# One hybrid layer on one core: h of the mLSTM branch transposed by VectorE through DRAM, gate stores on ScalarE's queue, row 5 of the modulation through yb's tiles, decay rows loaded a head ahead

## The chip, the core and the metric

The kernel runs on one core of a Trainium2 chip. A core has TensorE (PE, matrix products and transposes), VectorE (DVE), ScalarE (ACT), GpSimd (POOL) and SyncE (SP); each works through its own queue in order, and they wait for one another by semaphores. SP, ACT and POOL can issue DMA transfers, which 16 DMA engines carry out. The metric is the device time of one execution in microseconds (us), less is better; the comparison is by medians of repeated runs.

## The reference

One layer of a language model in float32: sequence 512, width 1024. A feed-forward part, then a mixing part with two branches (an mLSTM of 4 heads, and attention of 16 heads with a forget gate), then a second feed-forward part. Nine modulation rows come from a small product with w_ada. Cut to what matters here:

```python
def mlstm_chunkwise(q, k, v, i_pre, f_pre):
...
def forgetting_attention(q, k, v, f_pre, q_g, k_g):
...
    q = jnp.moveaxis(rms_norm(q, q_g), 1, 2)
    k = jnp.moveaxis(rms_norm(k, k_g), 1, 2)
...
    F = jnp.moveaxis(jnp.cumsum(jax.nn.log_sigmoid(f_pre.astype(f32)), axis=1), 1, 2)
...
        logits = jnp.einsum('bhqd,bhkd->bhqk', q_blk, k).astype(f32) * scale + (F_blk[..., :, None] - F[..., None, :])
        logits = jnp.where(k_pos[None, :] <= q_pos[:, None], logits, -jnp.inf)
        p = jax.nn.softmax(logits, axis=-1)
...
def hybrid_layer(...):
    mod = jax.nn.silu(c) @ w_ada + b_ada
    sh1, sc1, g1, sh2, sc2, g2, sh3, sc3, g3 = [m[:, None, :] for m in jnp.split(mod, N_MOD, axis=-1)]

    u = rms_norm(x, ffn1_norm_g) * (1 + sc1) + sh1
    x = x + 0.5 * g1 * swiglu(u, ffn1_w_in, ffn1_w_out)

    u = rms_norm(x, mix_norm_g) * (1 + sc2) + sh2
    z = u @ w_mix + b_mix
...
    y_a = jax.nn.sigmoid(o_m) * rms_norm(h_m, mlstm_norm_g).reshape(B, S, MLSTM_V).astype(x.dtype)
    y_b = forgetting_attention(...)
    merged = jax.nn.sigmoid(g_a) * (y_a @ w_branch_a) + jax.nn.sigmoid(g_b) * (y_b @ w_branch_b)
    x = x + g2 * (merged @ w_out)

    u = rms_norm(x, ffn2_norm_g) * (1 + sc3) + sh3
    x = x + 0.5 * g3 * swiglu(u, ffn2_w_in, ffn2_w_out)
    return x
```

The sizes are D = 1024, SEQ = 512, 4 mLSTM heads of 128 (keys) and 256 (values), 16 attention heads of 64, feed-forward width 2816. The columns of w_mix give, in this order, q, k, v and o of the mLSTM, its two gates, q, k, v and the gate of the attention, and the gates g_a and g_b of the two branches.

## The kernel before

All 512 tokens stay on the chip. Activations of a gemm lie transposed (128 features x 512 tokens, 8 tiles uh/ul). Each float32 product is made of three passes on rounded halves, high and low (`mm3`, lines 139 to 143): a weight tile raw of 512 KB is loaded by SP (`raw`, L106, a ring of three), rounded by ACT to wh (L116), and VectorE makes the rest wl (L118). The first two matmuls of an `mm3` in `gemm_stat` read wh only, the third reads wl.

The mixing part, roughly 390 to 830 us, runs in stages. First the gates and the mLSTM's q and k (`qk_conv`), with v of the mLSTM (`v_mlstm`: g banks in PSUM are evacuated into vf, L1066, and split into vm). Beside it, row 5 of the modulation is summed: `ada_row` (L305) loads eight raw tiles of w_ada and accumulates each, times a column of c, into two tiles yb6 and yb7 (L320). Then the mLSTM: `mlstm_w` makes the weights W of a head, `mlstm_h` its output hn, normalised and scaled (L1135), and stored to DRAM as h_d (L1136), 128 KB at a time. Then the attention, 16 heads, in a software pipeline over n (run, the loop over 18): `fox_s(n)` makes the scores (S: loads of the decay row A, L1257; Am, L1260; reductions L1271 and L1275; exponentials L1279), `fox_o(n - 2)` the product with the values (L1327), `fox_p(n - 1)` the probabilities: scaling by 1/sum (L1289), transposes (L1297), and their split into Ph (ACT, L1295) and Pl (DVE, L1296). `fox_t(p)` makes q and k of a pair of heads: for the first group by TensorE from tk, for the others from fT, which VectorE has transposed in blocks of 32 x 32 (L1176) and DRAM and `blocks` (L1141) have put together.

Between these steps stand generators of gemm work: `advance(fill, n)` takes n steps. A step is half a gemm of 24 matmuls. While heads 0 to 11 run, the fill is `fox_qkv` of the next group and `gate` (L1365: tanh of a gate's gemm, stored to g_d by SP one step later, L1367). While heads 12 to 15 run, the fill is `y_a(m)`, m = 0 to 7: the gemm of o, its tanh th (L1342), the load of a 512 x 128 piece of h_d as ht (L1344), four transposes of ht by TensorE (L1347), ya = scaled copy of their bank (ACT, L1349), and ya times (th + 1) (DVE, L1350).

The order on each engine is not the program's order: a scheduler places instructions by readiness in its own model, and the program's order is its priority. PSUM has four banks g for gemms and four banks t for the rest.

## Time and profile before

| | |
|---|---|
| median of 3 runs | 1313.94 us (1313.6 to 1314.72) |
| the profiled execution | 1315.71 us |
| its span, from first to last instruction | 1313.9 us |
| granted TensorE clock, mean | 0.999 |
| TensorE matmul busy | 1298.1 us |
| VectorE, ScalarE busy | 959.3 us, 632.0 us |
| DMA traffic | 260.49 MB, 198 GB/s |

In the answers of the trace, a group of instructions is one line: line of the code, engine, operation, out<-in by the program's names, shape and count, then busy time in us and mean in ns of one, then idle time of the engine before them and what ended it. A window is start:end and length, the busy time of PE, PEld (weight loads), DVE, ACT and POOL with counts, the granted clock, the share of DMA and GB/s. A chain is read from the top down: start, length, what the end of the window waited for at that time.

### The profile page before, as it was taken

What the parts mean: (1) busy time and instruction counts of PE and PEld (TensorE: products, weight loads), DVE (VectorE), ACT (ScalarE), POOL (GpSimd) and SP (SyncE); (2) the same over time, 40 slices, a digit from 0 to 9 for tenths busy, and PEclk for the clock granted to TensorE, in tenths of its full rate; (3) what the DMA queues carried; (4) which work ended last, traced back from release to release, by engine and by line L of the source; (5) the groups of instructions that cost most, each with busy time, mean ns of one, the idle gap of its engine ahead of it and who ended that gap; (6) DMA issues with size and microseconds to landing.
All of it is one profiled execution on the core that took longest, in us unless ns stands there. A gap on an engine that the chain in (4) does not pass through costs nothing.

```text
span 1313.9 us, 17822 instructions
## 1 busy us (share of the span) xinstructions
PE 1298.1 (99%) x6297; PEld 1088.0 (83%) x6297; DVE 959.3 (73%) x1748; ACT 632.0 (48%) x1055; POOL 37.2 (3%) x57
## 2 busy tenths in 40 slices
PE   7999999999999999999999999999999999999998
PEld 6788888887889878888888888878898888888887
DVE  6877777478688887888889685668567556635787
ACT  5633232355476665557575675334372223223651
POOL 1000000000010101000000000003000000000000
PEclk9999999999999999999999999999999999999999
DMA  9999978464855635535446482777539768634574
GB/s 290 277 330 304 324 258 285 128 192 154 301 138 146 201 110 149 163 110 154 127 106 174 101 215 77 235 218 236 182 113 322 265 221 279 221 104 133 170 265 150
DMA packets 231562, 260.49 MB, mean 198 GB/s; under 512 B 40544, under 2 KB 172288, under 8 KB 231472
## 3 DMA queue, kind: packets, MB, share of 16 engines
q1 hardware_dynamic: 231088, 259.27, 63.6%
q8 instruction: 50, 0.82, 0.3%
q14 instruction: 40, 0.33, 0.1%
q0 software_dynamic: 320, 0.06, 0.0%
q10 hardware_dynamic: 64, 0.02, 0.0%
HBM read 220.43 MB, written 38.87 MB: 197 GB/s over the span
## 4 chain that ended last, share of the span: by engine, by line
PE 84%; DVE 6%; DMA 5%; ACT 2%; issue 1%; SPq 1%; ACTq 0%; POOL 0%; DVEq 0%; POOLq 0%
PE g L143 22%; PE g L142 22%; PE g L141 22%; PE t L142 4%; PE t L141 4%; PE t L143 4%; PE g L925 1%; PE t L1327 1%; DMA raw<-in_w_mix_dram 1%; DVE wl L118 1%; PE t L1297 1%; DMA raw<-in_w_ada_dram 1%; DMA raw<-in_w_branch_b_dram 1%; ACT wh L116 1%; PE t L1268 1%
## 5 line engine op out<-in xcount | busy, mean ns | idle before, releaser
L116 ACT ACTIVATE wh<-raw 128x1024 fp32r<-128x1024 f32 (+2 forms) x246 | 249.1, 1017 | 361.6 <-PE g L142 124.3
L118 DVE TENSOR_TENSOR wl<-raw,wh 128x1024 fp32r<-128x1024 f32 (+2 forms) x246 | 287.4, 1171 | 144.6 <-ACT wh L116 122.8
L141 PE MATMUL g<-uh,wh 128*128 128x512 f32 (+1 forms) x880 | 340.7, 387 | 0.0
L143 PE MATMUL g<-uh,wl 128*128 128x512 f32 (+1 forms) x880 | 339.4, 386 | 0.0
L142 PE MATMUL g<-ul,wh 128*128 128x512 f32 (+1 forms) x880 | 339.2, 385 | 0.0
L143 PEld LDWEIGHTS g<-uh,wl 128*128 128x128 f32 x880 | 165.3, 188 | 33.6
L141 PEld LDWEIGHTS g<-uh,wh 128*128 128x128 f32 x880 | 165.4, 188 | 32.9 <-issue 0.5
L142 PEld LDWEIGHTS g<-ul,wh 128*128 128x128 f32 x880 | 165.4, 188 | 32.5
L141 PE MATMUL g<-wh,uh 128*128 128x512 f32 (+1 forms) x256 | 97.0, 381 | 1.5 <-DVE vf L1066 1.3
L143 PE MATMUL g<-wh,ul 128*128 128x512 f32 (+1 forms) x256 | 96.6, 377 | 0.0
L142 PE MATMUL g<-wl,uh 128*128 128x512 f32 (+1 forms) x256 | 96.5, 377 | 0.1
L320 DVE SCALAR_TENSOR_TENSOR acc<-raw,ccol,acc 128x1024 f32<-128x1024 f32 (+1 forms) x56 | 56.8, 1031 | 36.3 <-DMA raw<-in_w_ada_dram 36.2
L142 PE MATMUL t<-wl,A 128*128 128x512 f32 x176 | 68.6, 390 | 0.0
L141 PE MATMUL t<-wh,A 128*128 128x512 f32 x176 | 68.6, 390 | 0.0
L141 PEld LDWEIGHTS g<-wh,uh 128*128 128x128 f32 x256 | 48.1, 188 | 10.8 <-DVE vf L1066 1.7
L143 PEld LDWEIGHTS g<-wh,ul 128*128 128x128 f32 x256 | 48.2, 188 | 9.1
L142 PEld LDWEIGHTS g<-wl,uh 128*128 128x128 f32 x256 | 48.2, 188 | 8.9 <-DVE wl L118 0.5
L143 PE MATMUL g<-yh,wl 128*128 128x512 f32 x128 | 50.2, 392 | 0.2
L141 PE MATMUL g<-yh,wh 128*128 128x512 f32 x128 | 49.8, 389 | 0.0
L142 PE MATMUL g<-yl,wh 128*128 128x512 f32 x128 | 49.8, 389 | 0.0
L1279 ACT ACTIVATE S<-S,mn 128x128 f32<-128x128 f32 (+1 forms) x64 | 35.5, 555 | 19.7 <-DVE mn L1275 9.8
L436 ACT ACTIVATE A<-E 128x768 fp32r<-128x768 f32 x22 | 18.6, 846 | 54.7 <-DVE E L435 54.7
(373 smaller groups left out, 2245.8 us busy)
## 6 DMA issues: line engine op xcount, KB each, us to landing
raw<-in_ffn_w_in_dram SPq DMA_DIRECT2D x82, 512.0 KB
raw<-in_w_ada_dram SPq DMA_DIRECT2D x56, 512.0 KB
raw<-in_w_mix_dram SPq DMA_DIRECT2D x46, 512.0 KB
sa<-in_ffn_w_out_dram SPq DMA_DIRECT2D x22, 512.0 KB
sb<-in_ffn_w_out_dram SPq DMA_DIRECT2D x44, 256.0 KB
ws<-sa SPq DMA_DIRECT2D x22, 512.0 KB
ws<-sb SPq DMA_DIRECT2D x44, 256.0 KB
raw<-ws SPq DMA_DIRECT2D x44, 256.0 KB
```

Of the source, the lines that this page charges most:

```text
L116: nc.scalar.activation(hi, src, AF.Copy)
L118: self.last_lo = nc.vector.tensor_tensor(lo, src, hi, op=SUB)
L141: pin(mm(ps, lh, rh, start=start, stop=False))
L142: pin(mm(ps, lh, rl, start=False, stop=False))
L143: self.last_mm = pin(mm(ps, ll, rh, start=False, stop=stop))
L320: nc.vector.scalar_tensor_tensor(a, r[:, s], c, a, op0=MUL, op1=ADD)
L436: nc.scalar.activation(A1[:, 0:3, :], E[:, 0:3, :], AF.Copy)
L925: pin(nc.tensor.matmul(acc_ps[b], (wl if p == 1 else wh)[:, b % 2, s], self.ul[k] if p == 2 else self.uh[k], start=k == 0 and p == 0, stop ...
L1268: nc.tensor.matmul(ps[:, :w], q[:, s], k[:, :w], start=True, stop=False)
L1279: nc.scalar.activation(S[:, ws], S[:, ws], AF.Exp, scale=-1.0, bias=m, accum_out=sm[:, qb:qb + 1])
L1297: tr = lambda b, c, qb, kb: nc.tensor.transpose(b[:, c:c + P], S[:, P_OFF[qb] + kb * P:P_OFF[qb] + (kb + 1) * P], self.ident)
L1327: nc.tensor.matmul(po[:, q0:], vt[:, kb, i, :], Px[:, o:o + T - q0], start=n == 1, stop=n == 8)
```

## The change

`ada_early` takes the place of `ada_row` for row 5: 16 loads of 128 x 512 into yb0 to yb3 (two alternating pairs), not through raw; its products on VectorE are tied behind the last weight split or the last Wl. The 16 scalings of hn go to ACT; VectorE then transposes each 128 x 512 tile in blocks of 32 x 32, in place, and 256 KB are stored one step later. `ht_load` brings a piece of h, transposed, by four loads in 128-byte pieces (`blocks`), one m ahead; y_a has no TensorE transposes, and its product on VectorE comes a step later. A gate's store is issued by ACT right behind the tanh. `fox_s(h)` loads the decay row of head h + 1. `fox_t(0)` and `fox_t(1)` come earlier among the fill steps.

```diff
@@ -320,6 +320,30 @@
...
+            yield
+
+    def ada_early(self, v, yb, bank):
+
+        nc, A, V = self.nc, self.A, self.nc.vector
+        parts = [(yb[6], slice(0, 512)), (yb[7], slice(512, D))]
+        def load(k):
+            r = yb[2 * (k % 2):2 * (k % 2) + 2]
+            for t, (a, s) in zip(r, parts):
+                nc.sync.dma_start(t, A["w_ada"][0, k * P:(k + 1) * P, v * D + s.start:v * D + s.stop])
+            return r
+        r = load(0)
+        yield
+        for k in range(NK):
+            now, r = r, load(k + 1) if k + 1 < NK else None
+            c = self.ccol[:, k:k + 1]
+            with self.tc.issue_after(self.tie.ins):
+                for t, (a, s) in zip(now, parts):
+                    if k == 0:
+                        V.tensor_scalar(a, t, c, None, op0=MUL)
+                    else:
+                        V.scalar_tensor_tensor(a, t, c, a, op0=MUL, op1=ADD)
+            if k == NK - 1:
+                self.ada_sum(v, parts, lambda: yb[5][0:2, :], bank)
             yield
 
     def ada_sum(self, v, parts, new_row, bank):
@@ -1104,17 +1128,18 @@
...
-            nc.vector.tensor_tensor(Wl[:, ws], W[:, ws], Wh[:, ws], op=SUB)
+            self.tie = nc.vector.tensor_tensor(Wl[:, ws], W[:, ws], Wh[:, ws], op=SUB)
         self.W[h] = (Wh, Wl)
 
     def mlstm_h(self, h, ip):
         nc, sp = self.nc, self.sp
         (Wh, Wl), (vh, vl) = self.W[h], self.vt[h]
         ss = sp.tile([P, NT], F32, name=self.nm("hs"), tag="hs", bufs=2)
-        hs = []
+        hs, h2s = [], []
         for tb in range(NT):
             if tb % 2 == 0:
                 h2 = ip.tile([P, 2, 256], F32, name=self.nm("hn"), tag="bc", bufs=4)
+                h2s.append(h2)
             ps = self.tbank()
             for sb in range(tb + 1):
                 o = W_OFF[sb] + (tb - sb) * P
@@ -1132,8 +1157,13 @@
         nc.vector.tensor_scalar(v, ss, 1.0 / 256, EPS, op0=MUL, op1=ADD)
         r = self.rsqrt(v, NT)
         for tb in range(NT):
-            nc.vector.tensor_scalar(hs[tb], hs[tb], r[:, tb:tb + 1], None, op0=MUL)
-            nc.sync.dma_start(self.h_d[tb * P:(tb + 1) * P, h * 256:(h + 1) * 256], hs[tb])
+            nc.scalar.activation(hs[tb], hs[tb], AF.Copy, scale=r[:, tb:tb + 1])
+            if tb % 2:
+                t = h2s[tb // 2].rearrange("p b n -> p (b n)")
+                nc.vector.transpose(t, t)
+                self.post(1, lambda t=t, b=tb - 1: nc.sync.dma_start(
+                    self.h_d[b * P:(b + 2) * P, h * 256:(h + 1) * 256].rearrange("(b p) n -> p b n", p=P),
+                    t.rearrange("p (b n) -> p b n", b=2)))
 
     def blocks(self, t, src):
 
@@ -1253,8 +1283,11 @@
 
         nc, sp = self.nc, self.sp
         q, k, kl = (t[h % 2] for t in self.qkt[h // 2])
-        A0 = ip.tile([P, T], F32, name=self.nm("A0"), tag="bc", bufs=4)
-        nc.sync.dma_start(A0, self.A_d[h:h + 1, :].to_broadcast([P, T]))
+        def bring(h):
+            t = ip.tile([P, T], F32, name=self.nm("A0"), tag="bc", bufs=4)
+            nc.sync.dma_start(t, self.A_d[h:h + 1, :].to_broadcast([P, T]))
+            return t
+        A0 = bring(h) if h == 0 else self.A0
         Am = ip.tile([P, T], F32, name=self.nm("Am"), tag="bc", bufs=4)
...
@@ -1278,6 +1311,8 @@
             ws = slice(o, o + (qb + 1) * P)
             nc.scalar.activation(S[:, ws], S[:, ws], AF.Exp, scale=-1.0, bias=m, accum_out=sm[:, qb:qb + 1])
         self.S[h] = (S, sm)
+        if h < 15:
+            self.A0 = bring(h + 1)
 
     def fox_p(self, h, ip):
 
@@ -1331,23 +1366,28 @@
         nc.vector.tensor_tensor(self.yb[2 * g + pr][rows, :], po[rows, :], tmp[rows, :], op=ADD)
 
 
+    def ht_load(self, m, ip):
+        t = ip.tile([P, T], F32, name=self.nm("ht"), tag="tok", bufs=4)
+        self.blocks(t, self.h_d[:, m * P:(m + 1) * P])
+        self.ht.append(t)
+
     def y_a(self, m, ap, ip):
         nc = self.nc
+        if m == 0:
+            self.ht = []
+            self.ht_load(0, ip)
         ps = self.gbank()
         w = self.w_stat(self.A["w_mix"][0], OM + m * P)
         self.gemm_stat(ps, w, 0, T, range(0, 4))
         yield
+        if m + 1 < NK:
+            self.ht_load(m + 1, ip)
         self.gemm_stat(ps, w, 0, T, range(4, 8))
         th = self.tmp(ip, "th")
         nc.scalar.activation(th, ps, AF.Tanh, scale=0.5, bias=self.hom[:, m:m + 1])
-        ht = ip.tile([P, NT, P], F32, name=self.nm("ht"), tag="tok", bufs=4)
-        nc.sync.dma_start(ht, self.h_d[:, m * P:(m + 1) * P].rearrange("(b p) n -> p b n", p=P))
-        b = self.tbank()
-        for tb in range(NT):
-            nc.tensor.transpose(b[:, tb * P:(tb + 1) * P], ht[:, tb, :], self.ident)
         ya = ap.tile([P, T], F32, name=self.nm("ya"), tag="qk", bufs=16)
-        nc.scalar.activation(ya, b, AF.Copy, scale=self.hmg[:, m:m + 1])
-        nc.vector.scalar_tensor_tensor(ya, th, 1.0, ya, op0=ADD, op1=MUL)
+        nc.scalar.activation(ya, self.ht[m], AF.Copy, scale=self.hmg[:, m:m + 1])
+        self.post(1, lambda: nc.vector.scalar_tensor_tensor(ya, th, 1.0, ya, op0=ADD, op1=MUL))
         self.ya[m] = ya
         yield
 
@@ -1364,7 +1404,7 @@
             th = self.tmp(ip, "tg")
         nc.scalar.activation(th, ps, AF.Tanh, scale=0.5, bias=self.hgg[:, 8 * i + m:8 * i + m + 1])
         if not keep:
-            self.post(1, lambda: nc.sync.dma_start(self.g_d[8 * i + m], th))
+            nc.scalar.dma_start(self.g_d[8 * i + m], th)
         yield
 
 
@@ -1534,15 +1574,17 @@
         self.qk = [None] * 8
...
-        early = self.ada_row(5, lambda: self.yb[6:8], lambda: self.yb[5][0:2, :], self.tbank)
+        early = self.ada_early(5, self.yb, self.tbank)
         self.ada = (s for v in (6, 7) for s in self.ada_row(v, new, row, self.gbank))
         with tc.tile_pool(name="gates", bufs=1) as mp:
...
+            next(early)
             for m in range(4, 8):
                 ps = self.gbank()
                 w = self.w_stat(w_mix, m * P)
+                self.tie = self.last_lo
                 next(early)
                 self.gemm_stat(ps, w, 0, T)
                 if m == 7:
@@ -1579,12 +1621,12 @@
             for h0, n, fill in ((0, 3, with_gates(self.v_mlstm(1, ip, ip), 1)), (2, 4, with_gates(self.fox_qkv(0, ip), 3))):
                 for f, h in ((self.mlstm_w, h0), (self.mlstm_w, h0 + 1), (self.mlstm_h, h0), (self.mlstm_h, h0 + 1)):
                     f(h, ip)
-                    for _ in range(n):
+                    for i in range(n):
                         advance(fill, 1)
                         if f == self.mlstm_w and h < 2:
                             next(early, None)
-                    if f == self.mlstm_h and h == 2:
-                        self.fox_t(0, yp)
+                        if f == self.mlstm_h and h == 2 and i == 1:
+                            self.fox_t(0, yp)
                 advance(fill, 99)
             for n in range(18):
                 if n % 4 == 0 and n < 16:
@@ -1594,11 +1636,14 @@
                 last = n >= 12
                 if n < 16:
                     self.fox_s(n, ip)
-                    advance(fill, 4 if n == 0 else 3 if n == 1 else 1 if last else 2)
+                    advance(fill, 4 if n == 0 else 1 if last else 2)
+                if n == 1:
+                    self.fox_t(1, yp)
+                    advance(fill, 1)
                 if n >= 2:
                     self.fox_o(n - 2, ip)
                     advance(fill, 1)
-                if n % 2 and n < 13:
+                if n % 2 and 1 < n < 13:
                     self.fox_t((n + 1) // 2, yp)
                     if n == 11:
                         self.fox_t(7, yp)
```

The last part of the attention stage on ScalarE, before (names: wh is the weight of the y_a gemm whose raw it reads, g a gemm's bank, S the scores of head 13, th the tanh):

```order
L116 ACTIVATE wh_7653<-raw_7651 128x1024
L1292 ACTIVATE Ph_7674<-ident 128x128
L1279 ACTIVATE S_7588,sm_7590<-S_7588,mn_7589 128x128
L116 ACTIVATE wh_7754<-raw_7752 128x1024
L1279 ACTIVATE S_7588,sm_7590<-S_7588,mn_7589 128x256
L1279 ACTIVATE S_7588,sm_7590<-S_7588,mn_7589 128x384
L116 ACTIVATE wh_7837<-raw_7835 128x1024
L1279 ACTIVATE S_7588,sm_7590<-S_7588,mn_7589 128x512
L1342 ACTIVATE th_7626<-g_7565,hom 128x512
L1349 ACTIVATE ya_7635<-t_7630,hmg 128x512
```

There the weights of the next three gemms (raw_7651, raw_7752, raw_7835) are split ahead of the tanh of y_a(1), whose bank is g_7565. After the change, from the tanh of y_a(1) (g_7569) on:

```order
L1389 ACTIVATE ya_7719<-ht_7619,hmg 128x512
L1387 ACTIVATE th_7636<-g_7569,hom 128x512
L1365 ACTIVATE yt_7649<-t_7640 64x512
L116 ACTIVATE wh_7655<-raw_7653 128x1024
L1312 ACTIVATE S_7723,sm_7725<-S_7723,mn_7724 128x256
L1328 ACTIVATE Pl_7810<-ident 128x128
L1312 ACTIVATE S_7723,sm_7725<-S_7723,mn_7724 128x384
L1312 ACTIVATE S_7723,sm_7725<-S_7723,mn_7724 128x512
L1389 ACTIVATE ya_7802<-ht_7700,hmg 128x512
L1387 ACTIVATE th_7717<-g_7652,hom 128x512
L1365 ACTIVATE yt_7780<-t_7771 64x512
L116 ACTIVATE wh_7754<-raw_7752 128x1024
```

The weight of y_a(2) (raw_7653) now stands behind the tanh of y_a(1), and that of y_a(3) (raw_7752) behind the tanh of y_a(2), each with yt between.

On VectorE, in the same place, before (S_7588 is head 13, Am_7855 head 15):

```order
L1275 ISA S_7588,mn_7589<-t_7608,A_1438_7584,mn_7589 128x384
L1275 ISA mn_7589 128x1
L118 TENSOR_TENSOR wl_7755<-raw_7752,wh_7754 128x1024
L118 TENSOR_TENSOR wl_7838<-raw_7835,wh_7837 128x1024
L1286 RECIPROCAL sm_7590<-sm_7590 128x4
L1260 TENSOR_TENSOR Am_7855<-A_1494_7853,maskF 128x512
L1289 TENSOR_SCALAR S_7588<-S_7588,sm_7590 128x128
L1350 SCALAR_TENSOR_TENSOR ya_7635<-th_7626,ya_7635 128x512
L1331 TENSOR_TENSOR yb_3661<-t_7638,yt_7647 64x512
L1289 TENSOR_SCALAR S_7588<-S_7588,sm_7590 128x256
L1289 TENSOR_SCALAR S_7588<-S_7588,sm_7590 128x384
L1289 TENSOR_SCALAR S_7588<-S_7588,sm_7590 128x512
```

Behind head 13's last reduction come the low halves of the weights of y_a(3) and y_a(4). After (S_7591 is head 13, wl_7573 the weight of y_a(1)):

```order
L1308 ISA S_7591,mn_7592<-t_7611,A_1411_7482,mn_7592 128x384
L1308 ISA mn_7592 128x1
L1331 TENSOR_TENSOR Pl_7678<-t_7681,Ph_7677 128x512
L1321 RECIPROCAL sm_7593<-sm_7593 128x4
L1324 TENSOR_SCALAR S_7591<-S_7591,sm_7593 128x128
L1324 TENSOR_SCALAR S_7591<-S_7591,sm_7593 128x256
L1324 TENSOR_SCALAR S_7591<-S_7591,sm_7593 128x384
L1324 TENSOR_SCALAR S_7591<-S_7591,sm_7593 128x512
L1293 TENSOR_TENSOR Am_7721<-A_1439_7617,maskF 128x512
L118 TENSOR_TENSOR wl_7573<-raw_7570,wh_7572 128x1024
L1331 TENSOR_TENSOR Pl_7678<-t_7688,Ph_7677 128x512
L1331 TENSOR_TENSOR Pl_7678<-t_7695,Ph_7677 128x256
```

Here the low half of y_a(1)'s weight follows the reductions, the scaling and the mask of head 13. On TensorE, after, at that place (t_7681 to t_7695 are the transposes of head 12, t_7726 the first scores of head 14, g_7569 is y_a(1)):

```order
L1332 MATMUL t_7681<-ident,S_7456 128x128 x4
L1332 MATMUL t_7688<-ident,S_7456 128x128 x4
L1332 MATMUL t_7695<-ident,S_7456 128x128 x2
L1301 MATMUL t_7726<-fk_7380,fq_7378 128x256
L1302 MATMUL t_7726<-klz_5502,fq_7378 128x256
L141 MATMUL g_7569<-uh_3271,wh_7572 128x512
L142 MATMUL g_7569<-ul_3279,wh_7572 128x512
L143 MATMUL g_7569<-uh_3271,wl_7573 128x512
```

TensorE goes from the transposes of head 12 to two score matmuls and then to y_a(1); in before, half a gemm stood ahead of these transposes and half a gemm behind them.

On VectorE where the g banks of the mLSTM's v are evacuated (vf), before:

```order
L320 SCALAR_TENSOR_TENSOR yb_3662<-raw_4368,ccol,yb_3662 128x512
L320 SCALAR_TENSOR_TENSOR yb_3663<-raw_4368,ccol,yb_3663 128x512
L118 TENSOR_TENSOR wl_4375<-raw_4372,wh_4374 128x1024
L320 SCALAR_TENSOR_TENSOR yb_3662<-raw_4390,ccol,yb_3662 128x512
L320 SCALAR_TENSOR_TENSOR yb_3663<-raw_4390,ccol,yb_3663 128x512
L320 SCALAR_TENSOR_TENSOR yb_3662<-raw_4448,ccol,yb_3662 128x512
L320 SCALAR_TENSOR_TENSOR yb_3663<-raw_4448,ccol,yb_3663 128x512
L1066 TENSOR_TENSOR vf_4238<-g_4132,bb_4124 128x512
L1071 TENSOR_TENSOR vm_4126<-vf_4238,vm_4126 128x256
L1071 TENSOR_TENSOR vm_4129<-vf_4238,vm_4129 128x256
L1066 TENSOR_TENSOR vf_4250<-g_4133,bb_4124 128x512
```

and after:

```order
L118 TENSOR_TENSOR wl_4377<-raw_4374,wh_4376 128x1024
L118 TENSOR_TENSOR wl_4455<-raw_4452,wh_4454 128x1024
L1090 TENSOR_TENSOR vf_4240<-g_4134,bb_4126 128x512
L1090 TENSOR_TENSOR vf_4252<-g_4135,bb_4126 128x512
L1095 TENSOR_TENSOR vm_4128<-vf_4240,vm_4128 128x256
L1095 TENSOR_TENSOR vm_4131<-vf_4240,vm_4131 128x256
L1095 TENSOR_TENSOR vm_4128<-vf_4252,vm_4128 128x256
L1095 TENSOR_TENSOR vm_4131<-vf_4252,vm_4131 128x256
L1090 TENSOR_TENSOR vf_4264<-g_4136,bb_4126 128x512
```

The products of row 5 (yb) are gone from the rows ahead of vf, and the weight wl_4455 has moved ahead of vf as well.

## The prediction

> **What bounds the kernel now.** I read the page first, then the windows, then the chain of waits around each window that lost time. The page, engines and chain:

> ```profile
> PE 1298.1 (99%) x6297; PEld 1088.0 (83%) x6297; DVE 959.3 (73%) x1748; ACT 632.0 (48%) x1055; POOL 37.2 (3%) x57
> ...
> PE 84%; DVE 6%; DMA 5%; ACT 2%; issue 1%; SPq 1%; ACTq 0%; POOL 0%; DVEq 0%; POOLq 0%
> ```

> TensorE sets the time. So only two things can change it: TensorE work that is removed or added, and stretches in which TensorE stands. All edits lie between 390 and 830 us. The windows (start:end, length, then busy time of PE, PEld, DVE, ACT, POOL, clock, DMA share, GB/s) show how little TensorE stands there:

> ```profile
> 460.00:470.00 10.00, 8.54 (x39) 6.43 (x39) 9.52 (x19) 6.35 (x15) 1.55 (x3) 1.00 0.64 181
> ...
> 540.00:550.00 10.00, 9.60 (x53) 8.07 (x52) 9.01 (x32) 6.87 (x15) 0.00 (x0) 1.00 0.41 114
> 550.00:620.00 70.00, 69.62 (x393) 60.68 (x392) 58.69 (x167) 43.22 (x94) 0.00 (x0) 1.00 0.55 156
> ...
> 680.00:690.00 10.00, 9.36 (x48) 7.56 (x47) 6.27 (x15) 7.90 (x16) 0.00 (x0) 1.00 0.70 221
> ...
> 770.00:780.00 10.00, 8.98 (x46) 7.28 (x45) 9.65 (x27) 7.68 (x18) 0.00 (x0) 1.00 0.95 248
> ...
> sum 540.00, PE 535.79 PEld 454.01 DVE 428.40 ACT 308.12 POOL 25.43; mean PE 48.71 PEld 41.27 DVE 38.95 ACT 28.01 POOL 2.31
> ```

> From 390 to 930 us it stands 4.21 us in all: 1.46 at 460, 0.40 at 540, 0.38 from 550 to 620, 0.64 at 680, 1.02 at 770. No removed wait can bring more than these; a new wait has no such ceiling. TensorE is covered here because the program's order gives it a gemm whenever attention waits, so the changed order decides.

> **What goes: transposes.** The chain of waits inside the last part of the attention stage (start, length, what) gives TensorE's and VectorE's paces:

> ```profile
> 754.20 4.40 DMA A<-A_d
> ...
> 759.31 0.60 DVE ya L1350
> ...
> 769.88 0.58 DVE Am L1260
> ...
> 772.01 1.07 DVE S L1289 x3
> 773.09 1.13 DVE wl L118
> ...
> 774.25 1.30 DVE Pl L1296 x2
> ...
> 775.59 0.39 PE t L1268
> ...
> 777.00 0.23 PE g L141
> ...
> 779.73 1.27 PE t L1327 x8
> ...
> 783.76 0.44 PE t L1347 x4
> 784.19 1.09 PE t L1297 x10
> ```

> Four transposes of ht take 0.44 us of TensorE; y_a has 8 × 4 of them, all gone: 8 × 0.44 = **−3.5 us**. They are certain, because TensorE was busy on both sides.

> In their place VectorE gets 8 STREAM_TRANSPOSE of 128x512 and loses 16 scalings, which ScalarE takes over:

> ```profile
> L1135 DVE TENSOR_SCALAR hn<-hn,rq 128x256 f32<-128x256 f32 x12 | 3.4, 346 | 0.0
> ...
> L1176 DVE STREAM_TRANSPOSE tk<-tk 128x512 f32<-128x512 f32 x4 | 2.6, 686 | 0.0
> ```

> 8 × 0.686 = 5.5 us against 16 × 0.346 = 5.5 us: nothing for VectorE, and 16 × about 0.4 us more for ScalarE (the row of a 128x256 Ph below), which is 48% busy. h is needed some 200 us later, so I cost this at 0; without that cover it would be one transpose per tile, 0.7 us.

> **What goes: the wait at 460 us.** The chain there:

> ```profile
> 450.31 6.88 DMA raw<-in_w_ada_dram
> ...
> 459.28 1.78 DVE yb L320
> 461.06 0.61 DVE vf L1066
> ...
> 463.50 1.13 DVE wl L118
> ...
> 465.31 0.61 DVE vf L1066
> ```

> The vf rows free g banks that TensorE waits for. They stand on VectorE behind products of row 5 (yb), and these wait for a 6.88 us transfer. The changed VectorE order has vf right behind the weights' wl, and row 5's late products behind those. Row 5 arrives as 16 half loads through yb's tiles, no longer through the ring of three raw tiles. Its last four products may now wait on VectorE during mLSTM's first head, with W's products queued behind them; those feed matmuls several us later. I take the whole 1.46 us: **−1.5**, bounds −2.0 (the matmul after the wait is drawn too long in the trace) and 0 (another wait takes its place).

> **What goes: the small waits, 540 to 690 us.** They sum to 1.42. fox_t(0) and fox_t(1) move earlier among gemms, decay rows are loaded a head ahead, and SP no longer stands for gate tanhs. I take half, **−0.7**, bounds −1.4 and +0.5: fox_t(0)'s transposes now come singly among g matmuls, each behind its own tk scaling.

> The gates' stores bear on the 1.02 us at 770. The waits of SP's queue:

> ```profile
> SPq L1367 <- ACT tg L1365: 34.9, 8, 15.0
> ```

> and the first load that ScalarE issues now, at the start:

> ```profile
> 0.75 0.58 ACTq L179 DMA_DIRECT2D rowsC<-in_c_dram  x1
> ```

> SP stood up to 15 us for a tanh, with the load of A behind it (the 4.40 us transfer at 754.20, late), and the weights behind that. On ScalarE's queue the store stands behind its own tanh and blocks nobody else. 14 issues of some 0.6 us cost an engine with half its time free. Bounds: −1.02, and +1 where a store must wait for an earlier transfer with weight splits behind it.
> [...]

> **What comes: y_a's order.** This is the largest term. In before, ScalarE and VectorE split the weights of y_a two or three ahead: wh of a later gemm stands ahead of the tanh of an earlier one. In the change, the wh and wl of the next gemm stand behind the tanh (th) of the gemm just finished. And heads 11 to 14 come on TensorE without gemm halves between: T(11), QK(13), PV(11), T(12), a first pair of QK(14), and only then y_a(1). (T: transposes of S; QK: scores; PV: values.) Every engine keeps its order, so the weights can't come early even if raw has landed. The durations, VectorE then ScalarE, in this stage:

> ```profile
> L1271 DVE CUSTOM_DVE_ANT_0 S<-t,Am 128x128 f32<-128x128 f32 x12 | 3.2, 286 | 0.2
> ...
> L1275 DVE CUSTOM_DVE_ANT_0 S<-t,A,mn 128x384 f32<-128x384 f32 x3 | 1.8, 612 | 0.0
> ...
> L1275 DVE CUSTOM_DVE_ANT_0 S<-t,A,mn 128x256 f32<-128x256 f32 x3 | 1.4, 478 | 0.0
> ...
> L1275 DVE CUSTOM_DVE_ANT_0 S<-t,A,mn 128x128 f32<-128x128 f32 x3 | 1.0, 346 | 0.0
> ```

> ```profile
> L116 ACT ACTIVATE wh<-raw 128x1024 fp32r<-128x1024 f32 x8 | 8.5, 1059 | 5.8 <-DMA raw<-in_w_mix_dram 3.8 <-PE g L142 1.9
> L1295 ACT ACTIVATE Ph<-t 128x512 fp32r<-128x512 f32 x8 | 4.3, 596 | 1.8 <-PE t L1297 1.8
> ...
> L1342 ACT ACTIVATE th<-g,hom 128x512 f32<-128x512 f32 x5 | 3.4, 677 | 0.2 <-ACT wh L116 0.2
> L1279 ACT ACTIVATE S<-S,mn 128x512 f32<-128x512 f32 x4 | 2.9, 715 | 0.1
> ...
> L1330 ACT ACTIVATE yt<-t 64x512 f32<-64x512 f32 x4 | 2.4, 594 | 0.1
> L1295 ACT ACTIVATE Ph<-t 128x256 fp32r<-128x256 f32 x4 | 1.6, 395 | 0.0
> ```

> First wait, before y_a(1). Zero is the end of y_a(0)'s gemm. Tanh ends at 0.95 (with issue and latency), Ph and ya at 1.55. Pl of T(11), three pieces (1.3 + 0.4): 3.2. Head 13's seven reductions, 4 × 0.286 + 0.346 + 0.478 + 0.612 = 2.6, less the overlap of neighbours, 2.2: 5.4. The last exponential (0.72, and 0.19 for its sum) follows the Ph of T(12): 6.5. Then reciprocal 0.2, four scalings 1.3, Am 0.6, wl 1.13: 9.75. TensorE has, up to the third matmul of y_a(1), which is the first to read wl: T 1.09, QK 1.3, PV 1.27, T 1.09, a pair 0.24, two matmuls 0.46 = 5.45. It stands **4.3**.
> Second, before y_a(2): tanh 0.75, yt to 1.3, wh to 2.3 after the gemm's end; TensorE has six score matmuls, 1.05. It stands **1.25**; wl then comes under PV(12).
> Third, before y_a(3): wh again at 2.3, TensorE has one PV matmul, T(13) and one score matmul, 1.4: 0.9; two matmuls and a score matmul later wl (3.45) is awaited for 0.55. Together **1.45**.
> y_a(4) has QK(15) and PV(13) to cover it: about 0. Fourth, before y_a(5): 2.3 against 0.76 of T(14), and 0.5 for wl: **2.05**. The last heads' gemms are covered again.
> Sum 9.05, against 1.02 now: **+8.0**. Bounds: +2 (waits of 3 in all, rival 1) and +12 (raw late as well, rival 2).

> Raw may be late because ht comes in 128-byte pieces, on SP ahead of the weights. What such pieces take is seen where 16 loads of fT run, 722 to 735 us:

> ```profile
> DMA packets 8820, 1.71 MB, mean 132 GB/s; under 512 B 8497, under 2 KB 8497, under 8 KB 8820
> ...
> fT<-t_d SPq DMA_DIRECT2D x16, 64.0 KB
> ```

> 8192 pieces in some 8.4 us; ht has 16384, about 2.1 us of all queues for each of 8 tiles, spread over more than 60 us. I cost it at 0: the splits above come later than the raws. Without that cover it is up to 8 × 1 us.
> [...]

> **Sum.** −3.5 − 1.5 − 0.7 + 8.0 = +2.3; for stores that wait on ScalarE and fox_t(0) together I add +0.4: **+2.7**. The profiled execution took 1315.71 us (span 1313.9), so it would take 1318.4. The median of the runs is 1313.94, which lies 1.8 below the profiled time; the changed kernel's median: **1316.6 us**, own range 1314 to 1320.

> **Rivals.**
> (1) Faster. The stretch 756 to 818 is kept covered: VectorE's chain there runs shorter than my sum, since much of it starts before tanh ends, and the waits come to 3 us or less instead of 9. For it: TensorE stood only 1.02 us in this stage although VectorE was nearly full (9.65 of 10). Against it: th, yt and wh stand in that order on one engine, and TensorE's own work between is counted. With waits of w the sum is w − 6.3, so from 3.7 us downwards the kernel is faster than before by over 0.2%; at 3 it is −3.3, and with all other waits gone too some −5: 1309 to 1311.
> (2) Clearly slower. The 16384 pieces hold back the raws of y_a, which ring of three and SP's order put behind ht and behind A's free buffer. For it: DMA was full when TensorE last stood (0.95 at 770). Against it: part of the burst there came from SP's standing. Price: 8 × 0.5 to 1 us over the forecast: 1320 to 1324.
> (3) No net change: waits of 5.5 to 7, which pay back what the transposes and the wait at 460 brought: 1313 to 1315. For it: any one of the four waits may be covered; against it: no row says which.

> **How the numbers follow.** Forecast 0.50, rival 1 0.26, rival 2 0.14, rival 3 0.10. A measurement of this kernel tells 0.2% (2.6 us) from no change. The forecast's own range straddles that bound (1316.6): 0.32 of it counts as slower, 0.18 as same. Rival 1 is faster, 0.24, or just within, 0.02. So faster 0.24, same 0.30, slower 0.46. Range 1309 to 1322.

> **What would show it.** Right: no matmul of t<-ident,ht; window 460 to 470 full; between y_a(0) and y_a(5) four gaps of TensorE, the first of 3 to 5 us, ended by wl on VectorE or wh on ScalarE, and wh's idle time ended by PE, not by DMA. Wrong: that stage full (rival 1), or wh there released by DMA raw (rival 2); or a new gap between 470 and 750 us.

## The result, and the profile after

The changed kernel takes 1322.14 us (median of 4 runs, 1321.73 to 1323.13) against 1314.23 before on the same chip (4 runs, 1313.6 to 1314.72). The ratio is 1.006, 95% interval 1.0048 to 1.0072: slower by 7.9 us, where +2.7 was forecast and the range ended at 1322. The span grew from 1313.9 to 1320.5. One later execution of the changed kernel took 2180.42 us at a granted clock of 0.557; the ratios below leave it out.

The page of the changed kernel, its engines:

```profile
PE 1299.1 (98%) x6265; PEld 1087.7 (82%) x6265; DVE 959.1 (73%) x1740; ACT 639.4 (48%) x1072; POOL 36.8 (3%) x57
```

TensorE has 32 instructions fewer (the transposes of ht, listed before as x6297) and yet is busy 1 us longer. That is the first hint that some matmuls ran slowly. The windows of the changed kernel (columns as in the prediction):

```profile
460.00:470.00 10.00, 10.00 (x49) 8.50 (x48) 8.80 (x19) 5.27 (x15) 0.67 (x2) 1.00 0.28 86
470.00:540.00 70.00, 68.23 (x354) 57.27 (x354) 60.02 (x166) 42.66 (x99) 3.63 (x4) 1.00 0.45 131
...
680.00:690.00 10.00, 10.00 (x53) 8.51 (x52) 7.09 (x12) 5.78 (x10) 0.00 (x0) 1.00 0.71 190
...
760.00:770.00 10.00, 7.25 (x27) 5.32 (x26) 5.02 (x12) 4.92 (x11) 0.00 (x0) 0.83 0.86 180
770.00:780.00 10.00, 8.57 (x41) 6.99 (x40) 6.69 (x21) 5.17 (x11) 0.00 (x0) 1.00 0.44 84
780.00:790.00 10.00, 8.69 (x44) 7.01 (x43) 4.26 (x8) 5.04 (x11) 0.00 (x0) 1.00 0.46 79
790.00:800.00 10.00, 8.85 (x46) 7.18 (x45) 6.49 (x21) 6.53 (x14) 0.00 (x0) 1.00 0.20 52
800.00:810.00 10.00, 9.17 (x34) 7.23 (x35) 4.33 (x6) 4.40 (x9) 0.00 (x0) 0.83 0.38 107
...
sum 540.00, PE 529.02 PEld 446.26 DVE 423.94 ACT 313.41 POOL 25.48; mean PE 31.12 PEld 26.25 DVE 24.94 ACT 18.44 POOL 1.50
```

The waits at 460 and 680 are gone. TensorE now stands 1.77 us from 470 to 540, where it stood not at all, and 0.83 to 2.75 us in each of the windows from 760 to 810. The clock column says 0.83 in two of them. Idle time between 390 and 930 is 10.98 us against 4.21.

Progress says it without idle times, which hide slow matmuls. The starts of five TensorE instructions cut the span; they are the first transpose of xn in the mixing part, the first product of mLSTM head 0's W, the first score matmul of attention heads 0 and 12, and the first matmul of branch a. Differences of those starts, us:

| from, to (start in the kernel before) | before | after | difference | forecast |
|---|---|---|---|---|
| transposes of xn (372) to W of head 0 (459) | 86.88 | 86.95 | +0.1 | 0 |
| W of head 0 to scores of head 0 (551) | 91.99 | 92.45 | +0.5 | −1.5 and a part of −0.7 |
| scores of head 0 to scores of head 12 (749) | 197.48 | 196.19 | −1.3 | the rest of −0.7 |
| scores of head 12 to branch a (827) | 78.54 | 87.68 | +9.1 | −3.5 + 8.0 |
| branch a to the end | 486.78 | 486.68 | −0.1 | 0 |

They sum to +8.3. The first 372 us were 1.7 shorter in the profiled run after, with equal work there; in the other kernels' profiles they were 0.1 to 1.9 shorter, so nothing is read from them. Two places went wrong: the y_a stage by 4.6, the mLSTM stage by about 2.

**The y_a stage, first the waits.** A timeline of TensorE in the changed kernel, only the rows with idle time before them (start, length, what, then the idle time and what ended it):

```profile
756.58 0.38 PE L1301 MATMUL t<-fk,fq 128*128 128x256 f32 x1 [0.78 <-DVE Pl L1331]
761.39 0.39 PE L1301 MATMUL t<-fk,fq 128*128 128x256 f32 x1 [0.76 <-DVE Pl L1331]
762.92 0.51 PE L141 MATMUL g<-uh,wh 128*128 128x512 f32 x1 [1.03 <-ACT wh L116]
764.62 0.79 PE L143 MATMUL g<-uh,wl 128*128 128x512 f32 x1 [0.97 <-DVE wl L118]
773.95 0.51 PE L141 MATMUL g<-uh,wh 128*128 128x512 f32 x1 [1.43 <-ACT wh L116]
782.99 0.39 PE L1301 MATMUL t<-fk,fq 128*128 128x256 f32 x1 [0.90 <-DVE yb L1366]
784.48 0.51 PE L143 MATMUL g<-uh,wl 128*128 128x512 f32 x1 [0.40 <-DVE wl L118]
800.55 0.50 PE L141 MATMUL g<-uh,wh 128*128 128x512 f32 x1 [1.71 <-ACT wh L116]
801.81 0.54 PE L143 MATMUL g<-uh,wl 128*128 128x512 f32 x1 [0.28 <-DVE wl L118]
```

Four groups, at the four places forecast: 3.54, 1.43, 1.30 and 1.99, in sum 8.26. Six of the nine rows are ended by wh or wl. The other three, 2.44 us, are ended by Pl and yb, two other products of VectorE. What wh waited for stands in the groups of ScalarE from 750 to 820:

```profile
L116 ACT ACTIVATE wh<-raw 128x1024 fp32r<-128x1024 f32 x8 | 8.4, 1054 | 0.1
...
L1387 ACT ACTIVATE th<-g,hom 128x512 f32<-128x512 f32 x7 | 4.8, 689 | 19.8 <-PE g L143 19.8
```

ScalarE idled 0.1 us before wh, so no wh waited for its raw tile. It idled 19.8 us before the tanh, for the end of a gemm: wh stands behind the tanh, as forecast. The chain at the last of the four waits shows the loop whole:

```profile
797.85 0.24 PE g L143
...
798.12 0.69 ACT th L1387
...
798.83 0.59 ACT yt L1365
...
799.45 1.06 ACT wh L116
...
800.53 1.24 DVE wl L118
...
801.81 0.54 PE g L143
802.36 0.43 PE g L141
802.78 0.43 PE g L142
```

**Then the slow matmuls.** The last rows above are the second thing: behind the wait a matmul takes 0.43 us to the next instead of 0.23. There are 7 of them and a last one of 0.38 here, and 6 with one of 0.31 behind the wait at 764.62. Over what they would take that is 7 × 0.20 + 0.15 = 1.55 and 6 × 0.20 + 0.08 = 1.28, together 2.8 us.

### The profile page after: what moved, and what is told of

It reads as the page before. It is cut to its first block, busy times and chain, and to the rows that moved or that the text cites. A ratio compares the mean times of both kernels' runs of the same rounds, so it can differ in the third digit from the quotient of the medians.

```text
span 1320.5 us, 17784 instructions
## 1 busy us (share of the span) xinstructions
PE 1299.1 (98%) x6265; PEld 1087.7 (82%) x6265; DVE 959.1 (73%) x1740; ACT 639.4 (48%) x1072; POOL 36.8 (3%) x57
## 4 chain that ended last, share of the span: by engine, by line
PE 88%; DVE 6%; DMA 3%; ACT 1%; issue 1%; SPq 1%; POOL 0%; ACTq 0%; DVEq 0%; POOLq 0%
PE g L143 23%; PE g L141 23%; PE g L142 23%; PE t L141 4%; PE t L143 4%; PE t L142 4%; PE t L1362 2%; PE g L949 1%; DVE wl L118 1%; PE t L1332 1%; PE t L1302 1%; PE t L1301 1%; PE t L949 1%; ACT wh L116 1%; DVE x L609 1%
## 5 line engine op out<-in xcount | busy, mean ns | idle before, releaser
L116 ACT ACTIVATE wh<-raw 128x1024 fp32r<-128x1024 f32 (+2 forms) x246 | 248.8, 1016 | 364.8 <-PE g L142 111.2
L118 DVE TENSOR_TENSOR wl<-raw,wh 128x1024 fp32r<-128x1024 f32 (+2 forms) x246 | 287.0, 1170 | 147.0 <-ACT wh L116 127.0
L141 PE MATMUL g<-uh,wh 128*128 128x512 f32 (+1 forms) x880 | 342.4, 389 | 4.9 <-ACT wh L116 4.2
L142 PE MATMUL g<-ul,wh 128*128 128x512 f32 (+1 forms) x880 | 340.7, 387 | 0.0
L141 PEld LDWEIGHTS g<-uh,wh 128*128 128x128 f32 x880 | 166.1, 189 | 39.2 <-ACT wh L116 5.3
L142 PEld LDWEIGHTS g<-ul,wh 128*128 128x128 f32 x880 | 166.3, 189 | 32.8
L141 PE MATMUL g<-wh,uh 128*128 128x512 f32 (+1 forms) x256 | 97.4, 381 | 0.0
L142 PE MATMUL g<-wl,uh 128*128 128x512 f32 (+1 forms) x256 | 96.4, 376 | 0.0
L320 DVE SCALAR_TENSOR_TENSOR acc<-raw,ccol,acc 128x1024 f32<-128x1024 f32 (+1 forms) x56 | 57.0, 1032 | 46.8 <-DMA raw<-in_w_ada_dram 46.8
L141 PE MATMUL t<-wh,A 128*128 128x512 f32 x176 | 68.6, 390 | 0.0
L142 PE MATMUL t<-wl,A 128*128 128x512 f32 x176 | 68.5, 389 | 0.0
L142 PEld LDWEIGHTS g<-wl,uh 128*128 128x128 f32 x256 | 48.3, 189 | 8.3
L141 PEld LDWEIGHTS g<-wh,uh 128*128 128x128 f32 x256 | 48.2, 188 | 8.2
L142 PE MATMUL g<-yl,wh 128*128 128x512 f32 x128 | 49.9, 389 | 0.0
L141 PE MATMUL g<-yh,wh 128*128 128x512 f32 x128 | 49.8, 389 | 0.0
```

The source lines that it names most:

```text
L116: nc.scalar.activation(hi, src, AF.Copy)
L118: self.last_lo = nc.vector.tensor_tensor(lo, src, hi, op=SUB)
L141: pin(mm(ps, lh, rh, start=start, stop=False))
L142: pin(mm(ps, lh, rl, start=False, stop=False))
L320: nc.vector.scalar_tensor_tensor(a, r[:, s], c, a, op0=MUL, op1=ADD)
```

## The experiments

Twelve runs in three groups, each group on one chip with the kernel before beside it: 1316.01 us (18 runs, 1313.96 to 1318.31), 1315.07 (14 runs, 1313.75 to 1317.48) and 1315.18 (11 runs, 1313.51 to 1317.27). Where no ratio stands, there was one run. The lengths of the two stages that moved, and of the one between, cut as above:

| kernel | W of head 0 to scores 0 | scores 0 to 12 | scores 12 to branch a | span |
|---|---|---|---|---|
| before | 91.99 | 197.48 | 78.54 | 1313.9 |
| the change | 92.45 | 196.19 | 87.68 | 1320.5 |
| old_h_path | 92.29 | 196.20 | 76.90 | 1309.6 |
| old_row5 | 91.92 | 196.61 | 86.15 | 1319.5 |
| h_path_alone | 92.10 | 197.47 | 84.39 | 1319.0 |
| weights_ahead | 92.65 | 196.29 | 79.49 | 1312.6 |
| gates_ahead_too | 92.97 | 196.27 | 73.50 | 1308.0 |
| row5_early | 89.17 | 196.30 | 73.49 | 1315.6 |
| fill_the_wait | 91.97 | 196.27 | 78.24 | 1311.1 |
| gates_alone | 91.69 | 196.43 | 76.95 | 1309.5 |
| change_again | 92.48 | 196.28 | 87.61 | 1321.5 |
| no_row5_gates_ahead | 91.85 | 196.35 | 73.49 | 1308.2 |
| row5_two_sooner | 93.59 | 196.35 | 73.49 | 1309.4 |
| no_rows_ahead | 92.02 | 196.44 | 78.73 | 1312.1 |

**old_h_path: the change without its part on h** (transposes on TensorE again, ht in one load behind the tanh).

```diff
-            nc.scalar.activation(hs[tb], hs[tb], AF.Copy, scale=r[:, tb:tb + 1])
...
+            nc.vector.tensor_scalar(hs[tb], hs[tb], r[:, tb:tb + 1], None, op0=MUL)
...
-            self.ht_load(m + 1, ip)
...
+            nc.tensor.transpose(b[:, tb * P:(tb + 1) * P], ht[:, tb, :], self.ident)
```

> The change without its part on h: hn scaled by VectorE and stored as before, ht loaded in 512-byte pieces and transposed by TensorE; the other parts stay. Theory (the order of y_a comes from the loads of ht standing ahead of the weights): y_a has its half gemms between the attention steps, no slowed matmuls; the wait at 460 stays gone, and the new waits at 485 to 500 (2.3 us) stay if row 5's late products cause them: 1313 to 1315. Rival (the decay rows or the gates' stores made the order): it stays near 1322. Rival for the waits at 485 to 500 (the transposes of hn on VectorE cause them): they vanish, 1311 to 1312.5.

Measured 1312.02 us, ratio 0.9968 (0.9955 to 0.998). The stage took 76.90 us, with TensorE at 10.00 in every window from 750 to 830: without the part on h none of the four waits is there, although 32 transposes and the decay rows a head ahead are. The waits in mLSTM's first heads stay (0.86 us for vf, 0.93 us for hn), so the transposes of hn do not cause them.

**h_path_alone: the kernel before with that part alone** (the file also defines ada_early, which is not called).

> The kernel before with the part on h alone. Theory (its ht loads make the order, the decay rows a head ahead make it worse): gemms of y_a come whole, with one attention step or two between, so waits of 5 to 8 us in place of 10.4, against 3.5 us of transposes saved: 1316 to 1320. Rival (the order is bad only together with decay rows a head ahead): 1310 to 1313.

Measured 1320.05 us, ratio 1.003 (1.002 to 1.0041). The stage is slow here too, but for another reason. The chain of this kernel there:

```profile
754.78 0.43 SPq L1171
...
755.26 0.49 SPq L1171
...
757.38 5.95 DMA A<-A_d
...
763.97 1.23 DVE wl L118
```

and the first of the waits of SP's queue from 740 to 770:

```profile
SPq L1402 <- ACT tg L1400: 15.7, 2, 15.1
```

SP stands 15.1 us for a gate's tanh, since here the gates' stores are on its queue. Without the decay rows a head ahead, the row A then stands behind six issues for ht (L1171, some 0.5 us each) and one for a weight; it lands 5.95 us after its issue, and TensorE waits 3.41 us at 763.5. This is the late load of the second rival, only of A, not of raw, and not in the change. The loads of ht are not enough for it: in no_rows_ahead below, TensorE's order is the same and A also stands behind ht, but the stores are on ScalarE's queue, and no wait of the stage is longer than 0.78 us.

**old_row5: the change with row 5 summed as before.**

```diff
-        early = self.ada_early(5, self.yb, self.tbank)
+        early = self.ada_row(5, lambda: self.yb[6:8], lambda: self.yb[5][0:2, :], self.tbank)
...
-            next(early)
```

> The change without its part on row 5 (eight raw tiles, as before). If row 5's late products cause the waits at 485 to 500, these go (2.3 us) and the wait at 460 comes back (1.5 to 2 us): within 1 us of the change, 1321 to 1323. If the transposes of hn cause them, they stay and the wait at 460 comes on top: 1323.5 to 1325. The stage of y_a stays as in the change in both.

Measured 1321.57 us, ratio 1.0044 (1.0031 to 1.0056); the interval overlaps the change's. The wait at 460 is back (8.51 of 10 from 460 to 470), and 470 to 540 is full (70.00 of 70). The two cancel: 91.92 against 92.45 for the stage. The last stage has the same waits as the change, but one stretch of slow matmuls instead of two, and is 1.5 us shorter.

**weights_ahead: y_a's weights ahead of ht.** In the change a load of ht stands before the weights of the next gemm in the program. Here the weights are asked for two gemms ahead and before ht; ht still comes in its pieces, but each piece in its own m and no longer one m ahead.

```diff
-            self.ht_load(0, ip)
...
+        if m == 0:
+            self.ow = [self.w_stat(self.A["w_mix"][0], OM + j * P) for j in range(2)]
+        w = self.ow[m]
+        self.ht_load(m, ip)
...
-        if m + 1 < NK:
-            self.ht_load(m + 1, ip)
+        if m + 2 < NK:
+            self.ow.append(self.w_stat(self.A["w_mix"][0], OM + (m + 2) * P))
```

> The change with one thing different: in y_a the weight of the gemm two steps on is loaded and split ahead of the loads of ht, so on TensorE the half gemms again stand between the attention steps (QK, half gemm, PV, half gemm, T, half gemm); the 32 transposes of ht stay gone, ht still comes in 128-byte pieces. Theory (the order of y_a costs the time: 10.4 us of waits and about 3 us of slowed matmuls behind them): the stage from 745 to 825 us is full, and the time falls by 11 to 13.5 us against the change, to 1308.5 to 1311. Rival (the 128-byte pieces themselves hold up the weights): raw lands late, the waits stay, 1317 to 1323.

Measured 1315.65 us, ratio 1.0002 (0.9993 to 1.0011). From 750 to 800 TensorE is full; two windows of this kernel, then the chain further on:

```profile
760.00:770.00 10.00, 10.00 (x52) 8.45 (x51) 8.41 (x27) 7.03 (x16) 0.00 (x0) 1.00 0.83 179
...
810.00:820.00 10.00, 6.16 (x20) 4.62 (x21) 6.69 (x10) 7.15 (x12) 0.00 (x0) 0.83 0.46 131
```

```profile
810.27 0.72 ACT ya L1391
811.02 0.70 DVE ya L1392
811.74 0.63 ACT yh L1431
812.37 0.95 ACT wh L116
813.35 1.24 DVE wl L118
814.63 0.79 PE g L143
```

So the order in which the weights and h are asked for cost the four waits, and the small pieces did not. (The weights moved forward and h moved back in one edit; which of the two does it was not tried.) A new wait of 4.2 us stands at the next border: the first gate that is merged has its weights asked for only then, and wh stands behind ya and yh.

**gates_ahead_too: that, and the weights of the first two merged gates ahead as well.**

```diff
+        self.ow.append(self.w_stat(self.A["w_mix"][0], OM + (m + 2) * P if m + 2 < NK else GA + (m + 2 - NK) * P))
...
+        w = self.w_stat(self.A["w_mix"][0], (GA, GB)[i] + m * P) if th is None else self.ow[NK + m]
```

> weights_ahead, and the weights of the two gates that follow y_a are loaded and split inside y_a's steps as well. In weights_ahead TensorE stood 4.9 us at 810 us, until wl of the first gate, whose split stands behind tanh, ya and yh of y_a(7), and 9 matmuls behind that ran at the slow pace (about 1.4 us). Theory (only the place of the split is at fault): this wait goes, waits of at most 2 us are left between 745 and 830, and the time is 4 to 6.5 us under weights_ahead, 0.3 to 0.5% under before. Rival (the raw tile itself lands late there): the wait stays.

Measured 1309.78 us (1309.23 to 1310.34), ratio 0.9964 (0.995 to 0.9977): faster than both kernels. The stage takes 73.50 us, 5.0 less than before: 3.5 of transposes, 1.0 of waits, and some tenths of restarts. (Restart: the first matmul behind a wait, which is drawn longer, as the one of 0.51 us at 762.92 in the change against 0.39.) Of this 1.3 comes back behind the start of branch a (488.10 us from there to the end, against 486.78), mostly in a wait there: TensorE is busy 9.09 of 10 us from 820 to 830.

**fill_the_wait: weights_ahead with 20 extra matmuls in the wait**, into a bank that the next gemm overwrites. They add work and only keep TensorE busy.

```diff
+        if th is not None and m == 0:
+            for _ in range(20):
+                nc.tensor.matmul(ps, self.uh[0][:, 0:P], self.uh[0], start=True, stop=True)
```

> weights_ahead with 20 matmuls more (uh on uh into the bank of the first gate, overwritten by its gemm) in the 4.9 us in which TensorE stands at 810; the work is added, the result is the same. Theory (a stretch of idle TensorE lowers its granted clock, and the matmuls behind it pay 0.2 us each): the gemm starts at the same time and no matmul behind it is slow; granted clock 1.00 from 805 to 820, some 1.4 us less than weights_ahead. Rival (the slow matmuls come from what runs beside them, loads or splits): they are as slow as before.

Measured 1312.95 us, span 1311.1. Windows of weights_ahead, then of this kernel:

```profile
810.00:815.00 5.00, 1.16 (x3) 0.67 (x4) 3.04 (x5) 4.24 (x8) 0.00 (x0) 0.89 0.01 3
815.00:820.00 5.00, 5.00 (x18) 3.95 (x18) 3.65 (x6) 2.91 (x5) 0.00 (x0) 0.77 0.91 259
```

```profile
810.00:815.00 5.00, 4.99 (x23) 3.81 (x22) 3.80 (x6) 4.24 (x8) 0.00 (x0) 1.00 0.07 12
815.00:820.00 5.00, 5.00 (x24) 4.13 (x23) 4.89 (x8) 2.89 (x5) 0.00 (x0) 1.00 0.97 301
```

With the wait filled, the matmuls behind it run at 24 in 5 us instead of 18, at a clock of 1.00 instead of 0.77, and the stage is 1.25 us shorter with more work in it. So in this one execution the idle time is what made the matmuls behind it slow; the load of ScalarE, VectorE and DMA, which is the same or higher, did not.

**gates_alone: the kernel before with only the gates' stores on ScalarE's queue** (here too ada_early is defined and not called).

```diff
-            self.post(1, lambda: nc.sync.dma_start(self.g_d[8 * i + m], th))
+            nc.scalar.dma_start(self.g_d[8 * i + m], th)
```

> The kernel before with the gates' stores on ScalarE's queue alone. Theory (SP's standing for the tanhs delays A and the weights): the waits at 687 (0.97 us) and at 774 to 776 (1.35 us) go, 1.5 to 2.3 us less between QK(8) and the first branch. Rival (the decay rows loaded a head ahead remove them): they stay.

Measured 1311.38 us, span 1309.5 against 1313.9. Two windows of this kernel:

```profile
680.00:690.00 10.00, 10.00 (x52) 8.28 (x51) 8.10 (x14) 7.95 (x13) 0.00 (x0) 1.00 0.48 125
...
750.00:830.00 80.00, 80.00 (x415) 67.86 (x414) 57.13 (x127) 49.13 (x98) 0.00 (x0) 1.00 0.48 132
```

The waits at 680 and 770 are gone: −1.1 from scores 0 to scores 12 and −1.6 in the last stage by the table. Every kernel with this part has the middle stage at 196.2 to 196.6; the two without it, before and h_path_alone, have 197.5.

**row5_early: gates_ahead_too with two steps of row 5 for each of the four gemms of the mLSTM's k**, so that none is left behind 460.

```diff
                 next(early)
+                next(early, None)
```

> gates_ahead_too, and row 5 takes two steps ahead of each of the four gemms of the gates' stage, so that its last products come before vf and not in mLSTM's first head. Theory (the late products cause the waits at 487 to 501, 2.3 us): these go, 1.5 to 2.5 us less than gates_ahead_too. Rival: the products wait for their loads ahead of vf again, and a wait of 1 to 3 us appears between 450 and 470: no gain or a loss.

Measured 1317.76 us, ratio 1.002 (1.0011 to 1.0029): a miss. The waits of the mLSTM stage go (89.17), but the stretch ahead of it, from the transposes of xn to W of head 0, grows from 86.81 us in gates_ahead_too to 96.20: four waits come there, 3.40, 0.61, 0.57 and 1.63 us from 427 to 447, with slow matmuls behind the first. TensorE's timeline and the window of this kernel:

```profile
430.49 0.50 PE L143 MATMUL g<-uh,wl 128*128 128x512 f32 x1 [3.40 <-DVE wl L118]
```

```profile
430.00:440.00 10.00, 8.90 (x31) 6.85 (x32) 8.98 (x14) 2.85 (x5) 0.10 (x1) 0.83 0.79 235
```

**row5_two_sooner: gates_ahead_too with two more products of row 5 ahead of the last vf.**

```diff
                 if m == 7:
+                    next(early)
+                    next(early)
```

> gates_ahead_too with one more product of row 5 ahead of vf (five instead of four) and the last three in mLSTM's first head. Theory: the waits at 487 to 501 shrink by 0.5 to 1.5 us, none appears at 427 to 470. Rival: the extra load holds up a weight, a wait of over 1 us appears at 430 to 460.

Measured 1311.66 us, ratio 0.997 (0.9958 to 0.9982). The stage grew to 93.59: no gain. The edit takes two steps more, not the one that was expected; a wait of 1.00 us for vf at 464 is back, and one of 0.93 us stands at 482.

**no_row5_gates_ahead: gates_ahead_too with row 5 as before** (the edit of old_row5).

> gates_ahead_too with row 5 in eight raw tiles as in before. Theory (row 5's new way trades 1.96 us of waits at 460 for 2.3 to 2.9 us at 487 to 501): the waits at 487 to 501 go, those at 460 come back, within 1.5 us of gates_ahead_too, rather under it: 0.3 to 0.5% under before. Rival (row 5's new way is a gain in itself): 1.5 to 2.5 us more than gates_ahead_too.

Measured 1310.34 us (1309.47 to 1311.15), ratio 0.996 (0.9948 to 0.9972), the same as with row 5 through yb within the interval. In three forms row 5's products only moved the wait: 460, 487 to 501, or 427 to 447. VectorE is at 9.52 of 10 there before the change, and 14 products of 0.75 us have to go somewhere.

**no_rows_ahead: the change with each decay row loaded by its own head again.**

```diff
-        A0 = bring(h) if h == 0 else self.A0
+        A0 = ip.tile([P, T], F32, name=self.nm("A0"), tag="bc", bufs=4)
+        nc.sync.dma_start(A0, self.A_d[h:h + 1, :].to_broadcast([P, T]))
...
-        if h < 15:
-            self.A0 = bring(h + 1)
```

> The change without the decay rows loaded a head ahead. If the order of y_a gets worse by these rows, its waits fall from 10 us to 5 to 8.5 us as in h_path_alone, and the time is 1 to 4 us under the change; the waits at 687 and 774 stay gone, since they are due to the gates' stores.

Measured 1314.23 us, span 1312.1: 8.4 less than the change for one edit. In this kernel TensorE's order has gemm work between the steps of heads 11 to 14 again; its idle time in the stage is 2.7 us instead of 8.3, and no matmul of the stage is slow. So the four waits come from two things together: the change's order of h and weights, and the decay rows a head ahead. Without the first, TensorE does not stand in y_a at all (weights_ahead, old_h_path); without the second, it stands a third as long. With the rows a head ahead the scheduler, which places what is ready in its model, puts those heads' steps in a row; that this is why is argued from the orders, not tried alone.

**change_again: the changed kernel once more,** on another chip, to see whether the slow matmuls come again.

> The change unaltered, for a comparison on one chip with the next ones and for the pace of its matmuls. 0.5 to 0.7% over before. If the slow matmuls depend on where the stretch of idle falls in time and not on its length alone, the waits are the same to 0.1 us (4.4, 1.6, 1.6, 2.3) and the number of slow matmuls differs from the first profile (14 listed); if they depend on length alone, the same ones are slow.

Measured 1323.28 us, ratio 1.0056 (1.004 to 1.0072). The waits are the same to 0.02 us, and so are the two stretches of slow matmuls in the profiled execution. But one execution took 1319.86 us at a mean granted clock of 1.000, where four others took 1323.17 to 1324.93 at 0.997: some 3.4 us of the loss are not there in every execution. That it had no slow matmuls is inferred from its clock; there is no trace of it.

## Why the prediction missed

- **The direction, the places and most of the cause were right.** wh and wl stand behind the tanh, four groups of waits follow at the places named, and raw is never late: 3.54, 1.43, 1.30, 1.99 against 4.3, 1.25, 1.45, 2.05 forecast; in sum 8.26 against 9.05. But 2.44 of the 8.26 are waits for Pl and yb: 1.54 in the first group, which was forecast as one wait for wl, and 0.90 in the third, which was forecast as a wait for wh. That the sums agree so well is in part luck.
- **The step that failed is the sum of y_a's order, "Sum 9.05, against 1.02 now: +8.0".** It measured 9.1 + 3.5 = +12.6. It added idle time only. Left out were the slow matmuls, 2.8, and the restarts: a matmul is drawn 0.39 long and starts 0.23 after the one before it, so each of nine waits also loses some 0.16 of overlap (9 × 0.16 = 1.4, an estimate), and the first matmul behind six of them is drawn 0.50 to 0.79 instead of 0.39 (in sum 1.0). 8.26 + 2.8 + 1.4 + 1.0 = 13.5, less the 1.02: 12.4.
- **The clock was in no term.** No row of before shows a slow matmul behind a wait: the window with 1.46 us of waits at 460 has a clock of 1.00. The first wait, forecast as one of 4.3 us, came in pieces of at most 1.03 us, and the clock fell to 0.50 from 764.59 to 768.00 all the same. One execution of change_again, with a clock of 1.000, took 1319.86 us, which lies inside the range; so by how much the range was missed is partly luck.
- **"I take the whole 1.46 us: −1.5" failed**, by the bound named with it: another wait took its place. Rows of the VectorE products of row 5, before and after:

```profile
L320 DVE SCALAR_TENSOR_TENSOR yb<-raw,ccol,yb x8: 737/749/1783, 446.8 to 459.3; 128x512 f32<-128x512 f32 x8
```

```profile
L344 DVE SCALAR_TENSOR_TENSOR yb<-yb,ccol,yb x8: 745/746/751, 466.8 to 477.1; 128x512 f32<-128x512 f32 x8
```

  Eight instructions (two for each of the last four columns of c) now lie behind 466, 8 × 0.746 = 6.0 us of VectorE at the start of the mLSTM, to which the forecast gave no time. The sentence that those queued behind them "feed matmuls several us later" held for W's products, not for vf and hn, for which TensorE waits in the change:

```profile
488.23 0.50 PE L141 MATMUL g<-uh,wh 128*128 128x512 f32 x1 [0.76 <-DVE vf L1090]
499.24 0.41 PE L141 MATMUL t<-qkh,qkh 128*128 128x384 f32 x1 [0.72 <-DVE hn L1152]
500.66 0.36 PE L141 MATMUL t<-qkh,qkh 128*128 128x256 f32 x1 [0.30 <-DVE hn L1152]
```

- **The small waits** went a little further than forecast, −1.3 against −0.7, and the stores are why: alone they bring 2.6 us in the middle stage and the last. The row of SP's waits that the forecast weighed (34.9 us for gates' tanhs in 8 waits, the longest 15.0) was right: SP stood, with loads behind it.
- **The transposes** were sized right: in gates_alone and gates_ahead_too TensorE does not stand in the stage, and the one without the transposes is shorter by 76.95 − 73.50 = 3.45 us.
- **Rival 2's mechanism** is ruled out for the change by the row of wh, which waited 0.1 us, and by weights_ahead, which has the same pieces and is full up to 800; h_path_alone shows it for A, together with SP's standing. **Rival 1** came true only in other kernels, once the weights were moved.

In sum: y_a's order +4.6, row 5 about +2.0, the middle stage −0.6, and −0.4 for stores on ScalarE and fox_t(0), which were forecast as a cost and do not show, make 5.6, the difference between +8.3 and +2.7.

## What to carry to other kernels

Where a scheduler orders by readiness, ask of every early load what it stands ahead of in its queue: here 256 KB of h asked for before a weight tile, together with decay rows asked for a head ahead, turned a nearly full stage into one with four groups of waits, and asking for the weights first mended it. Before an edit is costed at nothing on an engine that is 95% busy in that window, find the wait that its work will cause next. Price a wait of the busiest engine at more than its idle time: the restart and the clock came to 5.2 us on top of 8.3 here.
